# Moving the matmul operands to other places within 128 bytes of SBUF

## The chip, the cores and the metric

The kernel runs on one core of one Trainium2 chip. The metric is the device time of one execution in microseconds (us), taken as the median of several runs. Profiles come from one further execution, so each profile has a time of its own that stands close to that median.

## The reference, cut to what matters

One layer of a diffusion backbone in float32: 256 latent tokens and 256 context tokens, 2048 features. Every sub-layer has an RMS norm and a shift, scale and gate that come from conditioning vectors.

```python
x   = half_ffn(x,   mx[0:3], ff1_norm, ff1_w_in, ff1_w_out)    # 2048 -> 2*5632 -> 2048
ctx = half_ffn(ctx, mc[0:3], ff1_norm, ff1_w_in, ff1_w_out)
hx  = modulate(rmsnorm(x, mix_norm), mx[3], mx[4])
q, k, v, bg, cg, u = split(hx @ w_in)                          # 2048 -> 6144
...                                                            # keys and values of ctx too
attn = neighbourhood_attention(q, k, v, kc, vc, rpb)
conv = gated_short_conv(bg, cg, u, conv_w, conv_b)
y = concat([rmsnorm(attn), rmsnorm(conv)]) @ w_out             # 2048 -> 2048
x = x + mx[5] * y
x = half_ffn(x, mx[6:9], ff2_norm, ff2_w_in, ff2_w_out)        # latent tokens only
```

Nearly all the arithmetic is in products of a 128-row slab of weights with 512 (or, for the latent tokens alone, 256) token columns.

## The kernel before

**Split operands.** Each float32 weight and each float32 activation is split into a high part (rounded to the chip's float32r form) and a low part (the rest). A product is then made of float32r matmuls: high by high, high by low, low by high. `mm3` (lines 196 to 200) does this for 512 tokens with three matmuls of 512 columns. `mm3_latent` (202 to 207) does it for 256 tokens with two: one of 512 columns, in which the high and the low part of the activations follow each other, and one of 256 columns. Each matmul has its own load of a 128x128 stationary tile, which TensorE does while the matmul before it runs.

**Weights.** The class `Weights` (55 to 97) feeds all of this. `_load` brings 128x1024 float32 values (512 KB) into one of four `wraw` buffers; `_split` copies them on ScalarE into a `whi` buffer (line 83) and takes the difference on VectorE into a `wlo` buffer (line 84). There are three `whi` and three `wlo` buffers, used in turn; 656 such tiles are split in the whole kernel. Each tile is used by eight 128-column slices, so its slices lie 512 bytes apart.

**Stages.** In time order: a start with the first modulation vectors (to about 150 us); the first feed-forward layer (`mm3`, lines 198 to 200, to about 1510 us), queries, keys and values (`mm3`, where the activations are stationary and the weights move) and the attention beside it; the convolution's products `bcu` and the output projection `wo` (`mm3_latent`, lines 206 and 207, to about 2030 us); and the second feed-forward layer (`mm3_latent`, to the end). In the feed-forward layers `ff_ab` is the first product (moving operand `h`), `ff_o` the second (moving operand `g`).

**Where things lie.** Pools are laid out one after another in each partition: constants, then the state with `x` and the sixteen activation tiles `h0` to `h15` (4096 bytes each), then the weights (four `wraw`, three `whi`, three `wlo`, 4096 bytes each), then the small tiles of the norms, then the pools of the stages, in which `g` lies. The sizes before are such that the start of every one of these large tiles is a multiple of 128 bytes: `h`, `wraw`, `whi`, `wlo` and `g` all lie at 0 modulo 128. The constant `nhalf` (line 159) takes 32 columns, of which at most eight are read.

**Order.** The program's order on TensorE is written out by hand; a small planner (`tick`, `go`) puts the attention's steps between the products. Nothing in it depends on addresses.

Of the kernel before, what the change touches and what calls it, by code (L numbers as in the profile page):

```python
# [11 lines left out]
F32 = mybir.dt.float32  # L12
F32R = mybir.dt.float32r
# [4 lines left out]
P = 128  # L18
# [15 lines left out]
RB = 2 * WIN_W - 1  # L34
BIG = 1.0e30
LEAD, LEAD2 = 8, 12
W_OUT = (range(7), range(7, 14), range(14, 16))
NRAW = 4
K_CB = 12
# [15 lines left out]
class Weights:  # L55


    def __init__(self, nc, pool, ahead_dma=3, ahead_split=2):
        self.nc, self.pool = nc, pool
        self.ad, self.asp = ahead_dma, ahead_split  # L60
        self.todo = deque()
        self.loaded = deque()
        self.ready = deque()

    def plan(self, aps, use=None):

        self.todo.extend((ap, use) for ap in aps)
# [8 lines left out]
    def _split(self):  # L76
        raw, n, use = self.loaded.popleft()
        if use is not None:
            use(raw)
            return  # L80
        hi = self.pool.tile([P, 1024], F32R, tag="whi", bufs=3, name="whi")
        lo = self.pool.tile([P, 1024], F32R, tag="wlo", bufs=3, name="wlo")
        self.nc.scalar.copy(out=hi[:, :n], in_=raw[:, :n])  # L83
        self.nc.vector.tensor_sub(lo[:, :n], raw[:, :n], hi[:, :n].bitcast(F32))  # L84
        self.ready.append((hi, lo, raw))
# [14 lines left out]
def build(nc, tc, ctx, I, out):  # L100
# [4 lines left out]
    cp = ctx.enter_context(tc.tile_pool(name="const", bufs=1))  # L105
# [5 lines left out]
    def bank(name):  # L111
        return ps.tile([P, 512], F32, tag="bank", bufs=8, name=name)
# [43 lines left out]
    nc.sync.dma_start(out=sel, in_=I["sel"])  # L156
    ones = cp.tile([P, P], F32, name="ones")
    dve.memset(ones, 1.0)
    nhalf = cp.tile([P, 32], F32, name="nhalf")
    dve.memset(nhalf, -0.5)  # L160

    sc = cp.tile([P, 2 * KT + 30], F32, name="sc")
# [234 lines left out]
    def ff_order(done, lead, together):  # L397

        order = [("in", f) for f in range(done, lead)]
        for c in range(0, NCH, together):  # L400
            cs = range(c, min(c + together, NCH))
            order.append(("out", cs))
            order += [("in", f) for f in range(lead + cs[0] * CH, min(lead + (cs[-1] + 1) * CH, NF))]
        return order

    def ff_plan(win, wout, order, also=lambda what: None):
        for what, i in order:
            if what == "in":
                gs = [win(2 * i + ab, hf) for ab in range(2) for hf in range(2)]
            else:  # L410
                gs = [wout[dp, c] for dp in range(KT // 2) for c in i]
            for g in gs:
                W.plan([g])
                also(what)
# [57 lines left out]
    W.plan([I["w_bcu"][i, hf] for ch in range(8) for i in (8 + ch, 16 + ch, ch) for hf in range(2)])  # L472
    W.plan([I["w_out"][d, hf] for dg in W_OUT for hf in range(2) for d in dg])
    ff_plan(lambda b, hf: I["ff2_w1"][b, hf], I["ff2_w2"], ff_order(0, LEAD2, 2))


    with ExitStack() as e1:
# [10 lines left out]
        with ExitStack() as e0:  # L488
# [62 lines left out]
            for k in range(KT):  # L551
# [8 lines left out]
                for n, b in enumerate((5, 0, 6, 1, 7, 2, 3, 4)):  # L560
# [10 lines left out]
                    else:  # L571
                        o = bank("ff_p")
# [63 lines left out]
    with ExitStack() as e2:  # L636
# [220 lines left out]
        stat = Stat(S, D, "s3")  # L857
        for dg in W_OUT:
            ob = {d: bank("wo") for d in dg}
# [147 lines left out]
```

## Time and profile before

| | |
|---|---|
| median of 3 runs | 2782.88 us (2780.96 to 2784.72) |
| the profiled execution | 2781.12 us |
| its span, first to last instruction | 2779.4 us |
| mean granted TensorE clock | 0.999 of full speed |
| TensorE matmul busy | 2767.5 us, 14236 instructions |
| VectorE busy, ScalarE busy | 1820.1 us, 964.8 us |

The span is what the profile explains; the remaining 1.7 us of the execution lie around it. A matmul's row has a modelled end, so its duration overlaps the next one's; what one matmul costs in a stream is read from the distance between two starts.

### The profile page before, as it was taken

The numbers are of one execution on the slowest core, as the hardware profiler recorded it, in microseconds if no ns is written. First come the engines' busy times: TensorE is split into PE (matmuls) and PEld (weight loads), VectorE is DVE, ScalarE is ACT, GpSimd is POOL, SyncE is SP. The second block draws the span as 40 slices with busy tenths as digits, with TensorE's granted clock in tenths as the row PEclk, the third lists the DMA queues.
The fourth block names the chain that finished last, engine by engine and source line by source line (L and its number), as shares of the span: only waits on it lengthen the run. The fifth ranks groups of instructions, "written<-read, shape, count | busy, mean of one in ns | idle before, by whom it ended". The sixth has DMA issues, their size and how long they took to land.

```text
span 2779.4 us, 36601 instructions
## 1 busy us (share of the span) xinstructions
PE 2767.5 (100%) x14236; PEld 2299.0 (83%) x14236; DVE 1820.1 (65%) x2944; ACT 964.8 (35%) x1338; POOL 57.6 (2%) x72
## 2 busy tenths in 40 slices
PE   9999999999999999999999999999999999999999
PEld 6788888888888888888888787888888888888888
DVE  5699866676665656566557836466875656565657
ACT  3222222222222222222224535454564444444443
POOL 0000000000000000000000102110000000000000
PEclk9999999999999999999999999999999999999999
DMA  9967645454566666555552433455555555555555
GB/s 343 348 207 224 208 153 180 143 182 142 184 198 199 200 200 194 191 195 192 193 179 84 133 95 117 134 156 174 189 166 184 189 184 188 185 186 188 184 189 167
DMA packets 158126, 510.41 MB, mean 184 GB/s; under 512 B 33408, under 2 KB 35968, under 8 KB 157824
## 3 DMA queue, kind: packets, MB, share of 16 engines
q1 hardware_dynamic: 157952, 508.08, 55.6%
q8 instruction: 111, 1.82, 0.3%
q14 instruction: 63, 0.52, 0.1%
HBM read 505.91 MB, written 2.10 MB: 183 GB/s over the span
## 4 chain that ended last, share of the span: by engine, by line
PE 91%; issue 3%; DVE 3%; DMA 2%; ACT 0%; POOL 0%; SPq 0%; DVEq 0%; ACTq 0%; POOLq 0%
PE ff_ab L206 12%; PE ff_ab L198 10%; PE ff_ab L199 10%; PE ff_ab L200 10%; PE ff_ab L207 6%; PE ff_o L206 6%; PE ff_o L200 6%; PE ff_o L198 6%; PE ff_o L199 6%; PE bcu L206 3%; PE ff_o L207 3%; PE wo L206 2%; PE bcu L207 2%; PE qkv L198 1%; PE qkv L200 1%
## 5 line engine op out<-in xcount | busy, mean ns | idle before, releaser
L83 ACT CAST whi<-wraw 128x1024 fp32r<-128x1024 f32 x656 | 689.1, 1051 | 1485.3 <-PE ff_ab L199 477.2
L84 DVE TENSOR_TENSOR wlo<-wraw,whi 128x1024 fp32r<-128x1024 f32 x656 | 801.7, 1223 | 476.1 <-ACT whi L83 466.5
L198 PE MATMUL ff_ab<-h,whi 128*128 128x512 f32 x1360 | 529.9, 390 | 0.0
L200 PE MATMUL ff_ab<-h,wlo 128*128 128x512 f32 x1360 | 529.4, 389 | 0.0
L199 PE MATMUL ff_ab<-h,whi 128*128 128x512 f32 x1360 | 529.3, 389 | 0.0
L206 PE MATMUL ff_ab<-h,whi 128*128 128x512 f32 x1344 | 475.2, 399 | 0.0
L207 PE MATMUL ff_ab<-h,wlo 128*128 128x256 f32 x1344 | 377.5, 281 | 0.0
L206 PEld LDWEIGHTS ff_ab<-h,whi 128*128 128x128 f32 x1344 | 252.6, 188 | 63.0
L344 DVE CUSTOM_DVE_ANT_0 area<-wraw,cb,half 128x1024 bf16<-128x1024 f32 x160 | 205.2, 1283 | 150.9 <-DMA wraw<-w_ada_t 150.3
L198 PEld LDWEIGHTS ff_ab<-h,whi 128*128 128x128 f32 x1360 | 255.5, 188 | 53.8 <-PE ada L513 0.4
L200 PEld LDWEIGHTS ff_ab<-h,wlo 128*128 128x128 f32 x1360 | 255.4, 188 | 53.5
L199 PEld LDWEIGHTS ff_ab<-h,whi 128*128 128x128 f32 x1360 | 255.4, 188 | 53.2
L344 DVE CUSTOM_DVE_ANT_0 area<-wraw,cb,prm 128x1024 bf16<-128x1024 f32 x160 | 205.2, 1282 | 113.2 <-DMA wraw<-w_ada_t 112.2
L200 PE MATMUL ff_o<-g,wlo 128*128 128x512 f32 x704 | 274.0, 389 | 0.1
L199 PE MATMUL ff_o<-g,whi 128*128 128x512 f32 x704 | 273.9, 389 | 0.0
L198 PE MATMUL ff_o<-g,whi 128*128 128x512 f32 x704 | 273.9, 389 | 0.0
L458 DVE SCALAR_TENSOR_TENSOR x<-ff_o,hgate,x 128x256 f32<-128x256 f32 x544 | 226.2, 476 | 64.7 <-PE ff_o L200 51.7
L207 PEld LDWEIGHTS ff_ab<-h,wlo 128*128 128x128 f32 x1344 | 253.9, 189 | 0.0
L206 PE MATMUL ff_o<-g,whi 128*128 128x512 f32 x704 | 249.0, 399 | 0.0
L207 PE MATMUL ff_o<-g,wlo 128*128 128x256 f32 x704 | 197.7, 281 | 0.0
L206 PEld LDWEIGHTS ff_o<-g,whi 128*128 128x128 f32 x704 | 132.3, 188 | 33.1
L200 PEld LDWEIGHTS ff_o<-g,wlo 128*128 128x128 f32 x704 | 132.1, 188 | 27.9 <-DVE wlo L84 0.5
(196 smaller groups left out, 2865.9 us busy)
## 6 DMA issues: line engine op xcount, KB each, us to landing
wraw<-ff_w SPq DMA_DIRECT2D x528, 512.0 KB, 3.3
wraw<-w_ada_t SPq DMA_DIRECT2D x224, 512.0 KB, 3.9
a<-w_ada_n SPq DMA_DIRECT2D x64, 512.0 KB, 6.9
wraw<-w_qkv SPq DMA_DIRECT2D x48, 512.0 KB, 3.4
wraw<-w_bcu SPq DMA_DIRECT2D x48, 512.0 KB, 3.3
wraw<-w_out SPq DMA_DIRECT2D x32, 512.0 KB, 3.8
x<-x SPq DMA_DIRECT2D x8, 512.0 KB, 6.7
bias<-rpb SPq DMA_DIRECT2D x64, 64.0 KB, 2.4
```

The lines of the kernel that those rows point to most:

```text
L83: self.nc.scalar.copy(out=hi[:, :n], in_=raw[:, :n])
L84: self.nc.vector.tensor_sub(lo[:, :n], raw[:, :n], hi[:, :n].bitcast(F32))
L198: pe.matmul(o, lhsT=wh, rhs=xh, start=first, stop=False, skip_group_check=True)
L199: pe.matmul(o, lhsT=wh, rhs=xl, start=False, stop=False, skip_group_check=True)
L200: pe.matmul(o, lhsT=wl, rhs=xh, start=False, stop=last, skip_group_check=True)
L206: pe.matmul(o2, lhsT=wh, rhs=x, start=first, stop=False, skip_group_check=True)
L207: pe.matmul(o2[:, 0, :], lhsT=wl, rhs=x[:, 0, :], start=False, stop=last, skip_group_check=True)
L344: dve.tensor_tensor_reduce(out=rows["junk"], in0=a, in1=rows["c"][:, v, h * 1024 : (h + 1) * 1024], scale=1.0, scalar=acc if h else bada(s ...
L458: dve.scalar_tensor_tensor(out=xs, in0=os_[d][:, c * S : (c + 1) * S], scalar=hgate[:, n, k, v : v + 1], in1=xs, op0=ALU.mult, op1=ALU.add)
```

## The change

The instructions, their order and their semaphores stay the same on every engine. Only addresses within a partition change.

```diff
+PLACES = (0, 4, 8, 12, 16, 20, 24, 2)
...
         self.ready = deque()
+        self.n = 0
...
-        hi = self.pool.tile([P, 1024], F32R, tag="whi", bufs=3, name="whi")
+        o = PLACES[self.n % len(PLACES)]
+        self.n += 1
+        hi = self.pool.tile([P, 1024 + 24], F32R, tag="whi", bufs=3, name="whi")[:, o : o + 1024]
         lo = self.pool.tile([P, 1024], F32R, tag="wlo", bufs=3, name="wlo")
...
-    nhalf = cp.tile([P, 32], F32, name="nhalf")
+    nhalf = cp.tile([P, 8], F32, name="nhalf")
```

`nhalf` is 96 bytes shorter, so all that is laid out behind it starts 96 bytes earlier: `x`, `h` and `wraw` go from 0 to 32 modulo 128. Each `whi` buffer is 96 bytes longer, so its three buffers start at 32, 0 and 96 modulo 128, and all behind them (`wlo`, the norms, the stages' pools with `g`) lie at 64. Within its buffer a `whi` tile starts 0, 16, 32, 48, 64, 80, 96 or 8 bytes in, in turn. Eight places by three buffers give eleven different starts modulo 128. Of the 656 tiles, counted in the built program, 84 start at 32, where `h` lies, 81 at 64, where `g` lies, and 82 at a start that is 8 modulo 16.

| modulo 128 | `h` | `g` | `wlo` | `whi` |
|---|---|---|---|---|
| before | 0 | 0 | 0 | 0 |
| after | 32 | 64 | 64 | 0, 8, 16, 32, 40, 48, 64, 80, 96, 104 or 112 |

## Rows read from the trace of the kernel before

**Rows 1.** The page: busy time of each engine (share, instructions), and granted clock.

```profile
PE 2767.5 (100%) x14236; PEld 2299.0 (83%) x14236; DVE 1820.1 (65%) x2944; ACT 964.8 (35%) x1338; POOL 57.6 (2%) x72
...
PEclk9999999999999999999999999999999999999999
```

**Rows 2.** The page: shares of the chain that ended last.

```profile
PE 91%; issue 3%; DVE 3%; DMA 2%; ACT 0%; POOL 0%; SPq 0%; DVEq 0%; ACTq 0%; POOLq 0%
```

**Rows 3.** Waits of TensorE: us in total, times, longest us.

```profile
PE ff_p L198 <- ACT h L311: 2.0, 2, 1.0
PE ff_p L199 <- DVE h L312: 1.7, 2, 0.9
```

**Rows 4.** Windows: length, then busy us (count) of PE, PEld, DVE, ACT, POOL.

```profile
150.00:1500.00 1350.00, 1349.88 (x5955) 1117.40 (x5954) 915.58 (x1428) 318.86 (x361) 0.00 (x0) 1.00 0.57 184
```

**Rows 5.** Timeline of TensorE, first feed-forward layer: start us, duration us.

```profile
700.34 0.39 PE L198 MATMUL ff_ab<-h,whi 128*128 128x512 f32 x1
700.57 0.39 PE L199 MATMUL ff_ab<-h,whi 128*128 128x512 f32 x1
700.79 0.39 PE L200 MATMUL ff_ab<-h,wlo 128*128 128x512 f32 x1
701.02 0.39 PE L198 MATMUL ff_ab<-h,whi 128*128 128x512 f32 x1
```

**Rows 6.** Timeline of TensorE, second feed-forward layer.

```profile
2299.91 0.40 PE L206 MATMUL ff_ab<-h,whi 128*128 128x512 f32 x1
2300.14 0.28 PE L207 MATMUL ff_ab<-h,wlo 128*128 128x256 f32 x1
2300.26 0.40 PE L206 MATMUL ff_o<-g,whi 128*128 128x512 f32 x1
...
2300.62 0.40 PE L206 MATMUL ff_o<-g,whi 128*128 128x512 f32 x1
...
2300.97 0.40 PE L206 MATMUL ff_o<-g,whi 128*128 128x512 f32 x1
```

**Rows 7.** Timeline of TensorE, output projection: first and last of 25 L206 rows.

```profile
1999.49 0.40 PE L206 MATMUL wo<-h,whi 128*128 128x512 f32 x1
...
2007.81 0.40 PE L206 MATMUL wo<-h,whi 128*128 128x512 f32 x1
```

**Rows 8.** The page: matmul groups; x is the count, then busy us, mean ns.

```profile
L198 PE MATMUL ff_ab<-h,whi 128*128 128x512 f32 x1360 | 529.9, 390 | 0.0
...
L206 PE MATMUL ff_ab<-h,whi 128*128 128x512 f32 x1344 | 475.2, 399 | 0.0
...
L198 PE MATMUL ff_o<-g,whi 128*128 128x512 f32 x704 | 273.9, 389 | 0.0
...
L206 PE MATMUL ff_o<-g,whi 128*128 128x512 f32 x704 | 249.0, 399 | 0.0
```

**Rows 9.** Timeline of TensorE: two float32 matmuls, each of two passes, and what follows.

```profile
1522.45 1.13 PE L281 MATMUL spread<-diag,ones 128*128 128x512 f32 x2
1523.02 0.80 PE L198 MATMUL qkv<-whi,uhi 128*128 128x512 f32 x1
...
1542.23 1.02 PE L626 MATMUL shiftb<-am,sel 128*128 128x512 f32 x2
1542.68 0.79 PE L198 MATMUL qkv<-whi,h 128*128 128x512 f32 x1
```

**Rows 10.** The page: the split of the weights on ScalarE and VectorE.

```profile
L83 ACT CAST whi<-wraw 128x1024 fp32r<-128x1024 f32 x656 | 689.1, 1051 | 1485.3 <-PE ff_ab L199 477.2
L84 DVE TENSOR_TENSOR wlo<-wraw,whi 128x1024 fp32r<-128x1024 f32 x656 | 801.7, 1223 | 476.1 <-ACT whi L83 466.5
```

## The prediction

> **What bounds the kernel now.** I read the page's busy times first. TensorE is busy through the whole span at its full clock, and its weight loads take 83%; VectorE and ScalarE are far below [rows 1]. The chain of work that ended last says the same: 91% of it is TensorE's, 2% a DMA's [rows 2]. The list of waits confirms that TensorE is never kept waiting for long: the two largest entries are 2.0 and 1.7 us in all [rows 3]. So the kernel's time is the number of matmuls times the distance from one start to the next, and the next view is the timeline of TensorE, read start to start.
>
> In the first feed-forward layer 5955 matmuls take 1350 us, 226.7 ns each [rows 4], and three of them go from 700.34 to 701.02, again 0.227 us each [rows 5]. [...]
>
> **What the change can touch.** No instruction is added, removed or moved, on any engine or queue, so there is no term for added work, and no wait is new. What changes is where TensorE reads: the stationary high parts at eleven places modulo 128 instead of one, against moving activations at 32 (`h`) or 64 (`g`), and low parts at 64. [...]
>
> The loads concerned: 1360 + 704 triplets in the first layer, with two high loads and one low load each, and 1344 + 704 = 2048 pairs in the second, with one of each [rows 8]. That is 2 x 2064 + 2048 = 6176 high loads and 4112 low ones. [...]
>
> Bounds of the unknown price. [...] Upward no row of this kernel has a matmul stream with worse placing. The nearest step that the rows show is 6.6 ns, the distance of the two rhythms; on every high load it is 6176 x 6.6 = 41 us. The least that a change of rhythm gives is the second layer alone going from 353.3 to 346.7 ns a pair: 2048 x 6.6 ns = 13.5 us.
>
> Is there a sign in the trace that the place or the pattern of a stationary read matters at all? One. Two float32 matmuls have the same moving shape, 512 columns in two passes, and differ in what is loaded as stationary: `ones`, 128 different columns, takes 1522.45 to 1523.02, 0.57 us; `sel`, one column read 128 times, takes 1542.23 to 1542.68, 0.45 us [rows 9]. With the read that stays at one address, 0.12 us is gone. That is few instructions, and of another type, but it speaks for a read that isn't free beside a moving operand.
>
> [...]
>
> What lies beside this: the split on ScalarE and VectorE writes and reads `whi` at the new places. A copy takes 1.05 us and a subtraction 1.22 us for a tile [rows 10], while 24 matmuls of a tile take 24 x 0.227 = 5.4 us in the first layer and eight pairs 8 x 0.353 = 2.8 us in the second. Even a subtraction twice as slow would be hidden, so I cost it at nothing; without that cover it would be 656 x 1.22 = 802 us, which is why I name it. The DMAs write `wraw` at 32 instead of 0; they were 2% of the chain and I cost that at nothing too.
>
> [...]
>
> **The sum.** I take the least of the gains: the steady rhythm of the second layer is one that its pairs fell into and that nothing disturbed for 700 us; with a new place at every tile of eight pairs it would be broken at each tile, and I expect the short one, as in the output projection. 13.5 us off the profiled span of 2779.4 us is 2765.9; with the 1.7 us around it 2767.6. The median before is 1.8 us above its profiled execution, so the forecast is 2769 us.
>
> **The rivals.**
> - *Nothing depends on the places.* [...] Against it: the two rhythms with equal instructions, and the 0.12 us. Time: 2783 us.
> [...]
> - *Slower: the new places meet more often.* The order before may be the favourable one: all at one place, each load in the same relation, and the first layer in the same 0.227 us throughout. With eleven places some relations are worse, and each tile needs a few pairs to settle. At 6.6 ns on half of the high loads it is 20 us, 2803 us; on all, 2824 us. It decides once the mean distance in the first layer is more than 0.9 ns above 226.7 ns (5.6 us over 6192 matmuls) and the second layer doesn't give it back.
>
> **How the numbers follow.** Chances: the short rhythm 0.32, 2769 us (its own range 2760 to 2778); nothing 0.29, 2783 us; the step gone 0.12, around 2711 us; slower 0.27, 2803 us. A time within 0.2%, 5.6 us, of 2783 counts as no change, which is about what this measurement can tell. That gives faster 0.44, same 0.29, slower 0.27. The range goes from 2700 us, a little below the step gone for most high loads, to 2824 us, the upper bound above.
>
> **What the profile after would show.** Rows of the first feed-forward layer at 226.7 ns and of the second at 346.7 ns make the forecast right step by step. The second still at 353.3 ns with all else equal means that nothing depends on places. [...] The forecast is wrong if the first layer moves at all, since the sum holds it fixed, and wrong in another way if TensorE begins to wait for `whi` or `wlo`.

## The result: slower by one per cent, and the profile after

The changed kernel takes 2808.57 us (three runs, 2808.46 to 2811.57) against 2782.88 us: a ratio of 1.0096, interval 1.0073 to 1.0119. The profiled execution took 2808.46 us, its span is 2806.7 us, 27.3 us longer than before. The forecast was 2769 us, faster.

The page of the changed kernel: span, busy times, and the shares of the chain that ended last.

```profile
span 2806.7 us, 36601 instructions
...
PE 2796.1 (100%) x14236; PEld 2298.6 (82%) x14236; DVE 1822.4 (65%) x2944; ACT 964.0 (34%) x1338; POOL 57.6 (2%) x72
...
PE 94%; issue 3%; DVE 2%; DMA 1%; POOL 0%; ACT 0%; SPq 0%; DVEq 0%; POOLq 0%; ACTq 0%
```

Beside [rows 1, 2] only one engine has changed: TensorE is busy 28.6 us longer with the same 14236 matmuls. Its weight loads, VectorE and ScalarE are within 2.5 us of before, and the clock row is full throughout, 0.999 of full speed on the mean in both. The list of TensorE's waits still begins with the two entries of [rows 3].

Waits of TensorE in the changed kernel.

```profile
PE ff_p L202 <- ACT h L315: 2.0, 2, 1.0
PE ff_p L203 <- DVE h L316: 1.7, 2, 0.9
```

So no wait has appeared; the same matmuls stand further apart. Two windows show where: 300 to 1500 us is the first feed-forward layer in both kernels, 2100 to 2740 us the second. Columns: length, then busy us and count of TensorE, its loads, VectorE, ScalarE, GpSimd; the last three are the granted clock, the busy share of the DMAs and GB/s. First the kernel before.

```profile
300.00:1500.00 1200.00, 1200.00 (x5295) 993.63 (x5295) 769.73 (x1188) 280.76 (x316) 0.00 (x0) 1.00 0.56 180
2100.00:2740.00 640.00, 640.00 (x3624) 555.01 (x3623) 389.24 (x528) 282.12 (x380) 0.00 (x0) 1.00 0.57 186
```

The same windows of the changed kernel.

```profile
300.00:1500.00 1200.00, 1200.00 (x5172) 971.20 (x5171) 743.22 (x1126) 263.71 (x287) 0.00 (x0) 1.00 0.54 178
2100.00:2740.00 640.00, 640.00 (x3666) 559.75 (x3666) 389.66 (x524) 288.20 (x395) 0.00 (x0) 1.00 0.57 189
```

Length by count: in the first layer a matmul went from 226.6 to 232.0 ns, 680 to 696 ns a triplet; in the second a pair went from 353.2 to 349.2 ns. The first starts of each stage give the balance.

| stage, by the first start of its matmuls | before, us | after, us | difference |
|---|---|---|---|
| start to the queries | 1507.5 | 1539.5 | +32.0 |
| queries, keys, values, attention | 259.2 | 262.6 | +3.4 |
| convolution, output projection, way into the second layer | 284.7 | 285.3 | +0.6 |
| second feed-forward layer | 723.9 | 715.3 | -8.6 |

The four differences are 27.4 us, the whole of it. Within the changed kernel the distance changes from tile to tile. Here are the first matmuls of triplets in the timeline around 632 us; by the program's order a tile whose high parts lie at the place of `h` begins at 626.30, one whose high parts lie 176 bytes (modulo 256) behind `h` at 631.90; the low parts lie 32 bytes behind `h` in both.

```profile
626.30 0.40 PE L202 MATMUL ff_ab<-h,whi 128*128 128x512 f32 x1
...
631.90 0.39 PE L202 MATMUL ff_ab<-h,whi 128*128 128x512 f32 x1
...
637.40 0.39 PE L202 MATMUL ff_ab<-h,whi 128*128 128x512 f32 x1
```

Eight triplets take 5.60 us, 700 ns each, and the next eight 5.50 us, 687 ns each. Neither is the 680 ns of [rows 5].

### The profile page after: what moved, and what is told of

Its sections match the earlier page's. It is cut to its first block, busy times and chain, and to the rows that moved or that the text cites. A ratio compares the mean times of both kernels' runs of the same rounds, so it can differ in the third digit from the quotient of the medians.

```text
span 2806.7 us, 36601 instructions
## 1 busy us (share of the span) xinstructions
PE 2796.1 (100%) x14236; PEld 2298.6 (82%) x14236; DVE 1822.4 (65%) x2944; ACT 964.0 (34%) x1338; POOL 57.6 (2%) x72
## 4 chain that ended last, share of the span: by engine, by line
PE 94%; issue 3%; DVE 2%; DMA 1%; POOL 0%; ACT 0%; SPq 0%; DVEq 0%; POOLq 0%; ACTq 0%
PE ff_ab L210 12%; PE ff_ab L203 11%; PE ff_ab L202 11%; PE ff_ab L204 11%; PE ff_ab L211 6%; PE ff_o L202 6%; PE ff_o L204 6%; PE ff_o L210 6%; PE ff_o L203 6%; PE bcu L210 3%; PE ff_o L211 3%; PE wo L210 2%; PE bcu L211 2%; PE qkv L202 1%; PE qkv L204 1%
## 5 line engine op out<-in xcount | busy, mean ns | idle before, releaser
L204 PE MATMUL ff_ab<-h,wlo 128*128 128x512 f32 x1360 | 535.1, 393 | 0.0
L348 DVE CUSTOM_DVE_ANT_0 area<-wraw,cb,half 128x1024 bf16<-128x1024 f32 x160 | 205.3, 1283 | 112.7 <-DMA wraw<-w_ada_t 111.8
```

What stands on the lines that cost most here:

```text
L204: pe.matmul(o, lhsT=wl, rhs=xh, start=False, stop=last, skip_group_check=True)
L348: dve.tensor_tensor_reduce(out=rows["junk"], in0=a, in1=rows["c"][:, v, h * 1024 : (h + 1) * 1024], scale=1.0, scalar=acc if h else bada(s ...
```

## The experiments

Two theories stood against each other first. *Relation*: the time depends on where the stationary tiles lie relative to the moving operand. *Turning*: a fixed place costs nothing, the change from tile to tile does. A third, *absolute*, held that a start off a multiple of 128 bytes, or at 8 modulo 16, has its own price. Places below are bytes of the high and of the low parts behind the moving operand, modulo 256, as (high, low). In the queries, where the weights move, the same shift stands between them and the activations.

**All shifted alike.** `nhalf` alone is shortened; everything lies at 32 modulo 128.

```diff
-    nhalf = cp.tile([P, 32], F32, name="nhalf")
+    nhalf = cp.tile([P, 8], F32, name="nhalf")
```

> Only the constant is cut from 32 to 8 columns: activations, high parts, low parts and g all lie at 32 modulo 128, in the same relation to each other as before, and nothing turns. Relation theory (the rhythm of the matmuls depends on where the loads lie relative to the moving operand): as before, triplets at 680 ns and pairs at 353 ns or 347 ns, 2783 us within 6 us. Absolute theory (a start that is not a multiple of 128 bytes costs by itself): the first feed-forward layer at 690 ns a triplet or more, at least 2800 us.

Measured: 2782.05 us against 2780.86 us, ratio 1.0003 (0.9993 to 1.0012). The windows of the first and second layer:

```profile
300.00:1500.00 1200.00, 1200.00 (x5295) 993.64 (x5295) 770.44 (x1182) 278.86 (x313) 0.00 (x0) 1.00 0.55 181
2100.00:2740.00 640.00, 640.00 (x3624) 554.98 (x3623) 389.06 (x528) 281.88 (x381) 0.00 (x0) 1.00 0.57 186
```

The counts are those of before, 5295 and 3624. The part of the change that moves the activations costs nothing as long as the weights move with them. The absolute theory falls, as far as one common shift, to 32 modulo 128, can show it.

**High parts alone, fixed 64 bytes off: (64, 0).** Pads ahead of and behind the three `whi` buffers; `half` is 32 bytes shorter to make room, which shifts everything alike.

```diff
+        self.n = 0
...
+        if not self.n:
+            self.pool.tile([P, 16], F32, tag="pad0", bufs=1, name="pad0")
         hi = self.pool.tile([P, 1024], F32R, tag="whi", bufs=3, name="whi")
+        if not self.n:
+            self.pool.tile([P, 48], F32, tag="pad1", bufs=1, name="pad1")
+        self.n += 1
...
-    half = cp.tile([P, 16], F32, name="half")
+    half = cp.tile([P, 8], F32, name="half")
```

> High parts at a fixed place 64 bytes off the activations and low parts, the same for every tile; activations, low parts and g keep one common place (96 modulo 128). Relation theory, from the tiles of the changed kernel that lie in this relation: triplets at 700 ns (680 before), pairs at 352 ns (353 before), so 2064 x 20 ns = 41 us in the first layer, some 6 us in the queries, -3 us in the second layer: about 2827 us. Turning theory (the change of place from tile to tile breaks the rhythm, a fixed one does not): 680 ns and 353 ns, 2783 us.

Measured: 2816.08 us, ratio 1.0123 (1.0106 to 1.0140). Window and timeline of its first layer:

```profile
300.00:1500.00 1200.00, 1200.00 (x5144) 966.40 (x5143) 742.87 (x1123) 262.33 (x286) 0.00 (x0) 1.00 0.55 178
```

```profile
699.93 0.40 PE L204 MATMUL ff_ab<-h,whi 128*128 128x512 f32 x1
...
701.33 0.40 PE L204 MATMUL ff_ab<-h,whi 128*128 128x512 f32 x1
```

Two triplets in 1.40 us, 700 ns each, fixed: nothing turns, and it is slower than the changed kernel. The turning theory falls. (The second layer came out at 350 ns a pair, less than the 352 expected; the sum expected was 2827 us.)

**A map.** High and low parts take 16 places each, 16 bytes apart, over 256 bytes.

```diff
+        self.n = 0
...
+        a, b = 4 * (self.n % 16), 4 * (self.n // 16 % 16)
+        self.n += 1
-        hi = self.pool.tile([P, 1024], F32R, tag="whi", bufs=3, name="whi")
-        lo = self.pool.tile([P, 1024], F32R, tag="wlo", bufs=3, name="wlo")
+        hi = self.pool.tile([P, 1024 + 64], F32R, tag="whi", bufs=3, name="whi")[:, a : a + 1024]
+        lo = self.pool.tile([P, 1024 + 64], F32R, tag="wlo", bufs=3, name="wlo")[:, b : b + 1024]
...
-                t = mp.tile([P, 4, P], F32, tag="pt", bufs=3, name="ptT")
+                t = mp.tile([P, 4, P], F32, tag="pt", bufs=2, name="ptT")
```

> A map: high parts at 16 places in steps of 16 bytes over 256 bytes, changing with every tile, low parts at the same 16 places, changing with every 16th tile; activations and g at 0. The last transposed tile of the attention has two buffers instead of three, to make room. Relation theory: triplets of a tile sit at steady values between 680 and 707 ns that depend on the two places, 680 where both are at 0; pairs between 340 and 361 ns; as a sum about that of the changed kernel, 2800 to 2815 us. If the places act modulo 128 alone, tiles that differ by 128 bytes in either place agree; if modulo 256, they differ. Absolute theory: tiles whose two places are equal but not 0 are as slow as the others, and the sum lies above 2800 us too.

Measured: 2807.93 us (one run; before 2780.86 us). Means of the eight triplets of a tile, from their starts, in ns; each value is one tile:

| high \ low | 0 | 16 | 64 | 128 | 144 |
|---|---|---|---|---|---|
| 0 | 683 | 698 | 692 | 694 | 680 |
| 16 | 681 | 700 | 693 | 700 | 681 |
| 64 | 699 | 700 | 700 | 692 | 707 |
| 144 | - | 700 | 693 | 700 | 681 |
| 240 | 695 | 680 | 697 | 693 | 681 |

Of 249 combinations none lies below 680; seven run at 680 once settled, all-equal among them. Equal places are not enough, since (64, 64) is at 700, so it is the moving operand that counts and not the high against the low parts alone. Tiles that differ by 128 bytes differ: (0, 0) has 683 ns and (0, 128) 694.

**Low parts alone, fixed 64 bytes off: (0, 64).** The pads of before around `wlo` instead of `whi`, with `half` 32 bytes shorter again.

```diff
+        if not self.n:
+            self.pool.tile([P, 16], F32, tag="pad0", bufs=1, name="pad0")
         lo = self.pool.tile([P, 1024], F32R, tag="wlo", bufs=3, name="wlo")
+        if not self.n:
+            self.pool.tile([P, 48], F32, tag="pad1", bufs=1, name="pad1")
+        self.n += 1
```

> The mirror of the run with the high parts moved: now the low parts alone lie 64 bytes off, fixed for every tile; high parts, activations and g share one place. Theory that any load off the moving operand's place breaks the triplet's rhythm: from the map's one tile in this relation, triplets near 692 ns instead of 680 and pairs near 347 ns, so 2064 x 12 = 25 us and some 4 us in the queries more, 2048 x 6 = 13 us less: about 2798 us. Theory that only the two high loads of a triplet matter: 680 ns, and a second layer between 347 and 353 ns: 2769 to 2783 us.

Measured: 2809.51 us, ratio 1.0102 (1.0085 to 1.0118). Its two windows:

```profile
300.00:1500.00 1200.00, 1200.00 (x5194) 974.87 (x5193) 750.08 (x1138) 266.38 (x292) 0.00 (x0) 1.00 0.55 179
2100.00:2740.00 640.00, 640.00 (x3624) 553.35 (x3623) 384.61 (x517) 284.94 (x390) 0.00 (x0) 1.00 0.57 186
```

1200 us by 5194 is 231.0 ns, 693 a triplet, as the map had it: moving one of three loads is enough. The second layer missed: 353.2 ns a pair, not 347, and the sum is 2809.51 us where 2798 was expected.

**Second layer, 32 combinations for eight tiles each.** From here on the second layer has weight buffers of its own, in a pool opened beside that of `g`.

```diff
+        if self.pool2 is None:
             hi = ...
             lo = ...
+        else:
+            a, b = PLACES[self.n // 8 % len(PLACES)]
+            self.n += 1
+            hi = self.pool2.tile([P, 1024 + 64], F32R, tag="whi", bufs=3, name="whi")[:, a // 4 : a // 4 + 1024]
+            lo = self.pool2.tile([P, 1024 + 64], F32R, tag="wlo", bufs=3, name="wlo")[:, b // 4 : b // 4 + 1024]
...
+        W.pool2 = e3.enter_context(tc.tile_pool(name="weights2", bufs=1))
```

> Up to the second feed-forward layer as before the change. In it the weights lie in a pool of its own, in which 32 pairs of places for high and low parts are held for eight tiles each (64 pairs of matmuls). Theory that a pair of places has one steady rhythm each: within eight tiles every combination settles at one value, some at 340 ns (by the map, high at 64 and low at 16; by the changed kernel, high at 192 and low at 0), most at 347 to 353. Theory that the rhythm depends on how the stream was entered as well: the same combination shows two rhythms in different tiles. The sum lies between 2765 and 2785 us.

Measured: 2770.05 us (one run; before 2780.81 us). Nearly every combination settled within a few pairs: 22 of the 32 at a mean of 346.6 to 347.2 ns, (192, 16) and (64, 240) at 340.1, (208, 0) and (128, 192) at 353.3. But (192, 0), at 340 in tiles of the changed kernel, ran at 350.0, and (0, 64) at 346.7 where the run before had 353.3 for a whole layer. So the places alone don't fix the rhythm. That the tile before has a part in it, the changed kernel shows: in its second layer the ten tiles at (96, 32) that follow one at (176, 32) have means of 343.1 to 343.2 ns a pair, the five that follow one at (200, 32) 352.0 to 352.1.

**The best place for the whole second layer: (192, 16).**

```diff
-PLACES = [(0, 0), (64, 0), ... (48, 96)]
+PLACES = [(192, 16)]
...
-            a, b = PLACES[self.n // 8 % len(PLACES)]
+            a, b = PLACES[self.n // 1 % len(PLACES)]
```

> First layer and everything up to the second feed-forward layer as before the change (all places equal). In the second layer the weights have buffers of their own, high parts 192 and low parts 16 bytes (modulo 256) off the activations, fixed. If the rhythm seen for this pair of places in eight tiles holds for the whole layer: 340.1 ns a pair instead of 353.3, so 2030 pairs x 13.2 ns = 27 us less: about 2755 us, faster than both kernels. If the rhythm depends on how the stream was entered, it may be 347 or 350 ns: 2768 to 2776 us.

Measured: 2755.18 us against 2781.87 us, ratio 0.9908 (0.9893 to 0.9922), faster than both kernels.

```profile
300.00:1500.00 1200.00, 1200.00 (x5296) 993.68 (x5295) 771.08 (x1187) 280.75 (x316) 0.00 (x0) 1.00 0.53 181
2100.00:2740.00 640.00, 640.00 (x3767) 566.65 (x3766) 410.53 (x564) 291.65 (x389) 0.00 (x0) 1.00 0.56 194
```

640 us by 1883.5 pairs is 339.8 ns, and the timeline has 24 pairs in 8.16 us, 340.0 ns:

```profile
2299.79 0.39 PE L214 MATMUL ff_o<-g,whi 128*128 128x512 f32 x1
...
2307.95 0.39 PE L214 MATMUL ff_o<-g,whi 128*128 128x512 f32 x1
```

**The control: the same buffers, all places equal.**

```diff
-PLACES = [(192, 16)]
+PLACES = [(0, 0)]
```

> Control: the second layer's weights in buffers of their own, but at the places of before (all equal). If the new buffers themselves change nothing: 353.3 ns a pair and 2782 us within 6 us; if the way into the layer decides the rhythm, 346.7 ns a pair and about 2769 us.

Measured: 2781.38 us, ratio 1.0001 (0.9991 to 1.0011); 353.2 ns a pair:

```profile
2100.00:2740.00 640.00, 640.00 (x3625) 555.00 (x3624) 390.24 (x530) 281.40 (x380) 0.00 (x0) 1.00 0.54 186
```

The new buffers do nothing; the gain is the places'.

**The other combination that ran at 340: (64, 240).** The diff differs in the two numbers.

> As the first kernel of this call, with high parts 64 and low parts 240 bytes off the activations, the second pair of places that ran at 340.1 ns a pair: 2755 us as well, or 2768 to 2776 us if the rhythm depends on the way in.

Measured: 2754.49 us (one run; before 2781.87 us), with the same count of matmuls in the window.

```profile
2100.00:2740.00 640.00, 640.00 (x3767) 566.64 (x3766) 411.10 (x565) 290.53 (x387) 0.00 (x0) 1.00 0.56 194
```

**First layer, 30 combinations for eight tiles each.** The edit of the map, with a list for `a, b` that moves on every eighth tile.

> Thirty pairs of places, each held for eight tiles, through the first layer, the queries and on (the transposed tile of the attention with two buffers). Theory that 680 ns is the floor of a triplet: no pair of places runs below 680, and those that the map had at 680 (0 and 144; 240 and 16; 16 and 0) hold it. Theory that the order before was only one good arrangement among better ones: some pair of places settles at 673 ns or less.

Measured: 2791.35 us (one run; before 2781.87 us). No combination went below 680: (0, 0), (16, 0), (240, 16), (16, 144), (144, 144), (240, 144) and (240, 240) held 680, all others lay at 686 to 698. One of the three that should have held missed: (0, 144), at 680 in its one tile of the map, ran at 697.8 here. The order before was already at the lowest rhythm found for triplets.

**High parts 8, 16 and 128 bytes off, fixed: (8, 0), (16, 0), (128, 0).** The first two by an offset of 2 or 4 words in a `whi` buffer of 1024 + 64 words, with `ptT` in two buffers; the third by two pads of 32 words, as in the run with 64.

> High parts fixed 8 bytes off the activations and low parts (which lie at 0), so that each load starts in the middle of 16 bytes; the last transposed tile of the attention has two buffers. Theory that a start at 8 modulo 16 has a price of its own: triplets above 700 ns, the slowest of the shifted places. Theory that only the rhythm counts: a steady value between 680 and 700 ns like the other places, 2783 to 2825 us.

> As the kernel before it in this call, with the high parts 16 bytes off. From the dwell run: triplets at 680 ns, as if nothing were shifted, so the first layer as before, and pairs at 350 ns in the second layer: about 2775 us. If any place off the activations' slows a triplet: 690 ns or more, 2800 us.

> High parts fixed 128 bytes off the activations and low parts, so modulo 128 all places are equal, as before the change. If the places act modulo 128: triplets at 680 ns, pairs at 347 to 353 ns, 2769 to 2783 us. If they act modulo 256, as the map's tiles 128 bytes apart suggest (694 ns in the one tile in this relation): triplets above 686 ns and at least 2790 us.

Measured, one run each: 2797.85, 2816.35 and 2821.47 us, with 2781.53 (first two) and 2781.04 us before. First layers of the three:

```profile
300.00:1500.00 1200.00, 1200.00 (x5194) 975.26 (x5194) 748.92 (x1138) 267.19 (x293) 0.00 (x0) 1.00 0.55 179
```

```profile
300.00:1500.00 1200.00, 1200.00 (x5144) 972.05 (x5143) 742.57 (x1123) 262.28 (x286) 0.00 (x0) 1.00 0.54 178
```

```profile
300.00:1500.00 1200.00, 1200.00 (x5145) 965.83 (x5144) 743.49 (x1123) 262.86 (x287) 0.00 (x0) 1.00 0.54 178
```

693, 700 and 700 ns a triplet; their second layers have 346.5, 349.8 and 351.8 ns a pair. A start at 8 modulo 16 shows no price of its own: 8 bytes off is quicker, at 693 ns, than 16 at 700, though slower than all equal at 680. And 128 bytes off, equal modulo 128, is among the slowest, at 700: to think of the places within 128 bytes was too short. My number for 16 bytes off, 2775 us, was wrong: (16, 0) held 680 for 64 triplets between two other combinations of the run before, and 700 for the whole layer when it was there from the start.

## Why the prediction was wrong

*What bounds the kernel* was right: no wait came or went, and the time is the distance of the starts.

*The step that failed* is the one that took "the least of the gains" and held the first layer fixed. It had two rhythms of the pairs with equal instructions, 353.3 and 346.7 ns [rows 6, 7], and then let only the layer move that stood in the longer one. But the first layer hangs on the places too, and it stood at the lowest rhythm that 249 combinations found, 680 ns. From there no place that was tried could gain. The three runs in which one kind of load is moved by 64 or 128 bytes show it: 693 and 700 ns. The price was 16 ns on each of 2064 triplets, 33 us by that sum and 32.0 us by the first starts up to the queries. The queries, the convolution and the output projection, which the sum left out, lost another 4.0 us.

The 2711 us that have the chance 0.12, and with them the lower end of the range, stand for a gain on most high loads that no run shows: the shortest triplets found have the 680 ns of before, and the fastest kernel takes 2754.49 us.

*The second layer* went the way forecast, but not as far: 4.0 ns a pair instead of 6.6, and 8.6 us instead of 13.5. New places at each tile did break the long rhythm, and brought a mixture of rhythms instead of the short one. Held at one good place, the same layer gives 13.4 ns a pair.

*The sign* that places matter at all, the 0.12 us between `ones` and `sel` of [rows 9], was misread. With the same `ones` loaded, two passes of 256 columns take 1905.12 to 1905.36, 0.24 us, close to half of the 0.45 us that `sel` takes for twice the columns.

```profile
1905.12 0.59 PE L281 MATMUL stat<-diag,ones 128*128 128x256 f32 x2
1905.36 0.59 PE L206 MATMUL bcu<-h,whi 128*128 128x512 f32 x1
```

What differs with `spread` is when its load began: with its matmul, at 1522.45. The loads of the other two, `sel` and this one, began ahead of their matmuls, by 0.23 and 0.11 us.

```profile
1522.45 0.30 PEld L281 LDWEIGHTS spread<-diag,ones 128*128 128x128 f32 x2 [0.84 <-issue]
1542.00 0.41 PEld L626 LDWEIGHTS shiftb<-am,sel 128*128 128x128 f32 x2
1905.01 0.31 PEld L281 LDWEIGHTS stat<-diag,ones 128*128 128x128 f32 x2
```

So the 0.12 us can't be put down to the way `ones` is read, and it was no sign of a dependence on places. That places matter was right, but it is the runs above that show it.

*The rivals.* "Nothing depends on the places" fell with the run at (64, 0). "Slower: the new places meet more often" has the direction, with its decision point reached (5.4 ns a matmul over the 0.9 named) and its 2803 us 6 us short; that places meet, no run shows. What spoke for it, the same 0.227 us throughout the first layer, would fit no dependence as well. What speaks for a dependence instead is that with nothing moved against the rest but a stationary operand, a triplet went from 680 to 700 ns.

*The eighth place* of the change, 8 modulo 16, shows no price by itself: with the high parts 8 bytes off a triplet ran at 693 ns, 16 bytes off at 700, all equal at 680, and a price of that start can't be told from one of places there.

*Left open*: what in the chip makes the rhythm, and by what rule a stream takes one of several that its places allow. That the place of the stationary tiles relative to the moving operand counts is shown, by 2782.05 us with all shifted alike and 2816.08 us with the high parts alone 64 bytes off; the way it does so isn't.

## What to carry to other kernels

In a stream of matmuls that waits for nothing, the distance of the starts is worth a look, stage by stage, for each form of matmul. Here the pairs stood at 353.3 ns in one stage and 346.7 in another [rows 6, 7], and a place gave 339.8; the triplets stood at 680 ns, and no place gave less. To find out, move the stationary tiles against the moving operand by multiples of 8 or 16 bytes over at least 256 bytes, hold each place for some tiles so that the rhythm settles, and read the starts; then fix the best place for that form and test it for the whole stage. Shifting all operands alike changed nothing in the one shift tried, 2782.05 us against 2780.86, and turning through places gave a mixture, 349.2 ns a pair where the best place has 339.8.

## What the runs showed of the hardware

Most distances come in steps. In the two runs that hold a combination of places for eight tiles, 21 of 30 settle at 680.0, 686.7 or 693.3 ns for a triplet of 3 x 512 columns, and 27 of 32 at 340.0, 346.7 or 353.3 ns for a pair of 512 and 256 columns, or at repeating patterns with such a mean. The step is 6.67 ns, and 700.0 ns, one step on, is the triplet of the fixed runs at (64, 0), (16, 0) and (128, 0). The others lie between, at 690.0 and 697.8 ns a triplet or 343.3 and 350.0 ns a pair, for example.

A rhythm can last a whole layer: in the run at (64, 0), all 1283 triplets of `ff_ab` from 156 us on have 699 or 700 ns by their starts, while in the window of 1200 us VectorE is busy for 742.87 us, ScalarE for 262.33 us and the DMAs for a share of 0.55. A shift of the high parts by 128 bytes counts, with 700 ns a triplet against 680, and one of all weights by 256 made no difference: in the run at (192, 16) the three buffers lie 4352 bytes apart, so that a tile's place changes by 256 bytes modulo 512, and the pairs have 340.0 ns in all of them.

And one relation can have two rhythms: all-equal pairs ran at 353.3 ns in the layer of the control and at 346.7 ns for 192 pairs in the run with 30 combinations.
